# Two decoder layers on one core: one stationary tile for the new tokens' high and low rows, and an opening of layer 0 in a fixed order

## The chip, the core and the metric

The kernel runs on one core of one Trainium2 chip. The metric is device time in microseconds (us) of one launch. Five engines work beside each other, each with its own queue of instructions in a fixed order: TensorE (PE) does the matrix products, ScalarE (ACT), VectorE (DVE) and GpSimd (POOL) do element-wise work, SyncE (SP) issues most of the DMA transfers; ACT issues some too. An instruction that waits holds up everything behind it in its queue.

## The reference

Two layers of a hybrid decoder, for 1024 prompt rows and 8 new tokens, 1024 channels. Each layer, cut to what matters here:

```python
h = rms_norm(x, norm_g)          # x / sqrt(mean(x^2) + eps) * g
(a_b, a_c, a_h, a_gate, s_q, s_k, s_v, s_gate, c_u, c_v, c_gate,
 d_q, d_k, d_v, d_gate) = split(h @ w_in)
# A: short gated convolution      B: sliding-window attention (s_q, s_k rotated; s_v)
# C: u * (tril(W_s) LN(v) + b)    D: dilated attention in three groups (d_q, d_k rotated; d_v)
branches = stack([y_a*silu(a_gate), y_b*silu(s_gate), y_c*silu(c_gate), y_d*silu(d_gate)])
x = x + sum(sigmoid(h @ w_merge) * (branches @ w_branch)) @ w_out
```

Everything is float32. The outputs are the last rms_norm of x for both request groups and the updated caches; the layer-normed rows of `c_v` of the new tokens are an output too.

## The kernel before

A product of full precision is made of three: each operand is split into a high part, rounded to the fast format of PE, and a low part, the rest; high x high, low x high and high x low are added in PSUM (`mm_cols`, and L372, L375, L376 in `tm_group`). A weight tile is split by `split_w`: two buffers for the raw load (`wr`), ACT takes the high part (`wh`, L154), POOL subtracts for the low part (`wl`, L156).

The activations stand channel-major: for each of 8 k tiles of 128 channels a tile of 1032 columns, first the 8 new tokens, then 1024 prompt rows. For layer 0 the scaled input is `h0h_k` (high) and `h0l_k` (low); 1/rms is not in them, since it is a factor per row that can be applied behind the products.

The opening of layer 0 makes these tiles (L250 to L265). The input comes in row tiles (`xin0` to `xin7`, `xs` for the new tokens). For three groups of row tiles (`GROUPS`: 0 to 2 with the new tokens, 392 columns; 3 to 5, 384; 6 and 7, 256) and each k, PE transposes the blocks into a PSUM tile (L259, L262), DVE copies them to `xT0_k` (L264), and `split_x` makes the high part on ACT (L207) and the low part on DVE (L209) or, for k = 1 and 5, by ACT and POOL (L213, L214). ACT then issues the store of `xT0` to `xres` (L267) and squares the input rows with a sum (L272) for the root mean squares. The first two channel-major products, `kB` and `qB0` (`rope_products`, L277 to L281), follow. The square root and the reciprocal give `rtok` (L325, L326); for the rotation tables 1/rms is spread over the partitions by products of a matrix of ones with diagonal tiles `dg` (L327 to L338).

Token-major products (`tm_group`) have the activations as the stationary operand: for 8 blocks of 128 rows and a ninth of the 8 new tokens, 24 products each. There are three such groups in a layer: the first v group (256 columns), `c_v` (384) and the second v group (256). ACT evicts each tile with the factor `rtok` (L391, L419).

PSUM tiles: `acc` has three buffers, `ms` three, `sc` one of two banks. A scheduler orders the instructions by their operands and places, so that the order of the program is not that of the queues; where the code says so, an instruction is kept in program order. Loads issued by `load` are held back to a few marked products ahead (`mark`).

## Time and profile before

| | us |
|---|---|
| median of three runs | 2382.03 |
| the three runs | 2382.03, 2385.53, 2381.37 |
| the profiled execution | 2387.34 |
| its span in the trace | 2385.6 |
| PE busy in the span | 2365.5 |
| DVE, POOL, ACT busy | 895.2, 843.5, 687.4 |

The rows come from one profiled execution, whose own time is 5.3 us over the median of the others. Its span is 1.7 us shorter than its time. A busy PE is not one at full rate: the granted clock is told beside the stretches where it counts. Starts of PE's instructions that follow each other are a better measure of a product's price than its duration, since products overlap.

### The profile page before, as it was taken

The page shows a single profiled execution, that of the slowest core. Times are in us where ns is not written, and L with a number is a line of the kernel's source. Part 1 is how long each engine was busy: PE and PEld are TensorE (multiplying, and loading weights), DVE is VectorE, ACT ScalarE, POOL GpSimd, SP SyncE. Part 2 cuts the span into 40 slices and gives each one's busy share as a digit, 9 for nine tenths or more (in the row PEclk, how much of TensorE's full clock was granted, in tenths as well). Part 3 has the DMA queues.
Part 4 walks back from the last instruction along what each step waited for, and adds up shares of the span by engine and source line. Part 5 has one row for each costly group of instructions (what it writes and reads, how often), then busy time and mean ns, then how long its engine had stood idle before and what let it go on. Part 6 is the DMA issues. An engine that isn't in the chain of part 4 may idle for free.

```text
span 2385.6 us, 38754 instructions
## 1 busy us (share of the span) xinstructions
PE 2365.5 (99%) x15896; PEld 2305.1 (97%) x15896; DVE 895.2 (38%) x1938; ACT 687.4 (29%) x1522; POOL 843.5 (35%) x556
## 2 busy tenths in 40 slices
PE   7999999999999999999999999999999999999999
PEld 6999999999999999999999999999999999999999
DVE  4345466335312222324333455554452221213143
ACT  5133432223212222223322244323231221212243
POOL 3333234432223444434442322353322233444330
PEclk9999999999899999999999999999989999999999
DMA  7342423433322212224542423244442122222232
GB/s 237 98 123 79 119 69 109 132 102 106 100 71 88 77 55 97 64 70 123 150 146 72 145 72 98 69 151 113 111 126 67 58 91 66 98 67 62 75 99 101
DMA packets 295962, 235.82 MB, mean 99 GB/s; under 512 B 52756, under 2 KB 279696, under 8 KB 293416
## 3 DMA queue, kind: packets, MB, share of 16 engines
q1 hardware_dynamic: 267952, 206.25, 28.8%
q10 hardware_dynamic: 27832, 27.10, 4.1%
q8 instruction: 124, 2.03, 0.4%
q14 instruction: 54, 0.44, 0.1%
HBM read 192.35 MB, written 76.47 MB: 113 GB/s over the span
## 4 chain that ended last, share of the span: by engine, by line
PE 98%; DVE 1%; DMA 0%; ACT 0%; SPq 0%; issue 0%; ACTq 0%; DVEq 0%
PE acc L181 27%; PE acc L182 27%; PE acc L178 27%; PE acc L372 2%; PE acc L375 2%; PE acc L376 2%; PE sc L540 2%; PE ms L569 2%; PE ms L558 1%; PE ms L733 1%; PE ms L479 0%; PE ms L1042 0%; DMA wr<-in_w_in_dram 0%; DVE xT L264 0%; DVE h0l L209 0%; PE ms L333 0%
## 5 line engine op out<-in xcount | busy, mean ns | idle before, releaser
L156 POOL TENSOR_TENSOR wl<-wr,wh 128x384 fp32r<-128x384 f32 (+2 forms) x228 | 476.9, 2093 | 827.3 <-ACT wh L154 698.7
L181 PE MATMUL acc<-h1l,wh 128*128 128x344 f32 x1584 | 511.5, 323 | 0.0
L182 PE MATMUL acc<-h0h,wl 128*128 128x344 f32 x1584 | 510.4, 323 | 0.0
L178 PE MATMUL acc<-h0h,wh 128*128 128x344 f32 x1584 | 509.3, 322 | 0.9 <-DVE xT L264 0.9
L178 PE MATMUL acc<-h1h,wh 128*128 128x344 f32 x1584 | 510.2, 322 | 0.0
L182 PE MATMUL acc<-h1h,wl 128*128 128x344 f32 x1584 | 509.5, 322 | 0.0
L181 PE MATMUL acc<-h0l,wh 128*128 128x344 f32 x1584 | 508.9, 321 | 0.0
L154 ACT ACTIVATE wh<-wr 128x384 fp32r<-128x384 f32 (+2 forms) x228 | 205.2, 901 | 421.4 <-PE acc L181 393.6
L1005 DVE TENSOR_TENSOR th<-acc,rr 128x344 f32<-128x344 f32 x192 | 99.1, 516 | 553.5 <-PE acc L182 553.5
L181 PEld LDWEIGHTS acc<-h1l,wh 128*128 128x128 f32 x1584 | 299.9, 189 | 4.2 <-issue 3.6
L181 PEld LDWEIGHTS acc<-h0l,wh 128*128 128x128 f32 x1584 | 299.2, 189 | 3.9 <-issue 3.5
L182 PEld LDWEIGHTS acc<-h1h,wl 128*128 128x128 f32 x1584 | 299.7, 189 | 2.8 <-issue 2.3
L178 PEld LDWEIGHTS acc<-h0h,wh 128*128 128x128 f32 x1584 | 299.1, 189 | 2.8 <-issue 1.2
L182 PEld LDWEIGHTS acc<-h0h,wl 128*128 128x128 f32 x1584 | 298.6, 189 | 2.9 <-issue 2.3
L178 PEld LDWEIGHTS acc<-h1h,wh 128*128 128x128 f32 x1584 | 299.6, 189 | 1.4 <-issue 1.0
L1011 POOL TENSOR_TENSOR mg<-mg,th 128x344 f32<-128x344 f32 x144 | 134.0, 931 | 303.3 <-DVE th L1010 303.3
L1006 ACT ACTIVATE th<-th 128x344 f32<-128x344 f32 x192 | 94.3, 491 | 496.9 <-DVE th L1005 496.4
L178 PE MATMUL acc<-yh,wh 128*128 128x344 f32 x576 | 184.4, 321 | 0.0
L182 PE MATMUL acc<-yh,wl 128*128 128x344 f32 x576 | 184.3, 320 | 0.0
L181 PE MATMUL acc<-yl,wh 128*128 128x344 f32 x576 | 184.1, 320 | 0.0
L181 PE MATMUL acc<-ml,wh 128*128 128x344 f32 (+3 forms) x384 | 123.2, 321 | 0.0
L182 PE MATMUL acc<-mh,wl 128*128 128x344 f32 (+3 forms) x384 | 123.0, 321 | 0.0
(278 smaller groups left out, 3256.6 us busy)
## 6 DMA issues: line engine op xcount, KB each, us to landing
wr<-in_w_merge_dram SPq DMA_DIRECT2D x64, 512.0 KB
out_dram<-in_cache_dil_kv_dram SPq DMA_DIRECT2D x128, 255.9 KB
wr<-in_w_in_dram SPq DMA_DIRECT2D x60, 512.0 KB
y<-yscr SPq DMA_DIRECT2D x18, 516.0 KB
wr<-in_w_branch_dram SPq DMA_DIRECT2D x48, 192.0 KB
wr<-in_w_in_dram SPq DMA_DIRECT2D x32, 256.0 KB
wr<-in_w_out_dram SPq DMA_DIRECT2D x16, 512.0 KB
out_dram<-in_cache_dil_kv_dram SPq DMA_DIRECT2D x16, 511.0 KB
```

The costliest lines, as they stand in the source:

```text
L154: act.activation(hi, raw, AF.Copy)
L156: pool.tensor_tensor(lo, raw, hi.bitcast(F32), op=ALU.subtract)
L178: mm = pe.matmul(ps[:, :n], hi[:, k], xh[k][:, cs], start=(k == 0), stop=False)
L181: pe.matmul(ps[:, :n], hi[:, k], xl[k][:, cs], start=False, stop=False)
L182: pe.matmul(ps[:, :n], lo[:, k], xh[k][:, cs], start=False, stop=(k == kt - 1))
L372: mm = pe.matmul(ps[:M, :N], lh, hi[:, k % kk], start=(k == 0), stop=False)
L375: pe.matmul(ps[:M, :N], ll, hi[:, k % kk], start=False, stop=False)
L376: pe.matmul(ps[:M, :N], lh, lo[:, k % kk], start=False, stop=(k == KT - 1))
L540: pin(pe.matmul(ps[:, h, a * 256:a * 256 + u.nk], u.qs[h], u.ks[h], start=True, stop=True))
L1005: dve.tensor_tensor(t, pg[:, :CH], rr[:, cs], op=ALU.mult)
L1006: act.activation(t, t, AF.Tanh, scale=0.5)
L1011: pool.tensor_tensor(mg[m][:, cs], mg[m][:, cs], t, op=ALU.add)
```

## The change

Four things change.

The first is in `tm_group`. The ninth tile of a group, for the 8 new tokens, uses a stationary tile `hd` of 40 rows for each k: rows 0 to 7 the high parts, rows 32 to 39 the low parts, zeros between. Two products per k (weight high, weight low) give both. ACT copies the lower rows (32 to 39) out of PSUM into `sd`, DVE adds the upper ones, and the consumer reads the sum.

The second is the order of the opening, written as turns (one k of one group) and steps, all of it kept in program order. The products of the first weight tile follow the turns two behind; those of the second come four k tiles later. The high part is scaled out of PSUM directly; for even k ACT copies the tile to `xT0` afterwards, for odd k DVE copies first; all low parts are DVE's. `busy` issues products of ones, whose result nobody reads, ahead of the first turns. Six of the squares and the first splits of v weights lie between the turns.

The third is the place of the `dg` products: behind the first v group. The fourth are small moves: the load of `wsp`, transposes pinned in program order, `attention()` ahead of the scores of the D decode, three first loads on ACT's queue.

```diff
+    def tm_weights(l, srcs, kk, k0):
...
-        act.activation(hi, raw, AF.Copy)
+        in_order(act.activation(hi, raw, AF.Copy))
...
+    idle = pacc()
+    def busy(n):
+        for _ in range(n):
+            in_order(pe.matmul(idle[:, :P], onesm, onesm, start=True, stop=True))
...
-    for n0, n1 in GROUPS:
+    def turn(n0, n1, k):
...
-        for k in range(KT):
-            ps = pmisc() if k % 2 else pacc()
...
-            dve.tensor_copy(xt, ps[:, :w])
-            split_x(0, k, cs, xt, (hh, hl), k % 4 != 1)
+        ps = pmisc()
...
+        if k % 2:
+            in_order(dve.tensor_copy(xt, ps[:, :w]))
+        split_x(0, k, cs, ps[:, :w], (hh, hl))
+        if k % 2 == 0:
+            in_order(act.activation(xt, ps[:, :w], AF.Copy))
...
+    def first_products(a, s):
+        c, k = s // KT, s % KT
+        if k == 0 and a == 0:
+            if c == 1:
+                accs.append([pacc(), pacc()])
+            else:
+                two = pscore()
+                accs.append([two[:, 0], two[:, 1]])
...
+        if k == KT - 1:
+            done.append(lambda: in_order(act.activation(kq0[a][:, cs], ps, AF.Copy)))
+
+    LAG = 4
+    squares = (7, 9, 12, 14, 17, 19)
+    for s in range(3 * KT + LAG):
+        if s == 0:
+            for t in turns[:2]:
+                turn(*t[0], t[1])
+                busy(4)
+            split_first(0, 0)
+        if s in (2, 3, 6):
+            split_first(*{2: (0, 1), 3: (1, 0), 6: (1, 1)}[s])
+        if s + 2 < len(turns):
+            turn(*turns[s + 2][0], turns[s + 2][1])
+        while done:
+            done.pop(0)()
+        if s in (18, 22):
+            w_v.append(tm_weights(0, V_FIRST, 4, 4 * len(w_v)))
+        if s in squares:
+            square(squares.index(s))
+        if s < 3 * KT:
+            first_products(0, s)
+        if s >= LAG:
+            first_products(1, s - LAG)
+    for n in range(6, 9):
+        square(n)
+    while done:
+        last = done.pop(0)()
+    opening[0] = False
+    behind_opening = ExitStack()
+    behind_opening.enter_context(tc.issue_after(last.ins))
     for k in range(KT):
         act.dma_start(xres[0][k], xT0[k])
...
+                if n == 8:
+                    for k in range(KT):
+                        for a, w in enumerate(ws[k // kk]):
+                            pe.matmul(ps[:40, :N], hd[:, k], w[:, k % kk], start=(k + a == 0), stop=(k + a == KT))
+                    s = tp.tile([NS, MIX], F32, tag="ct", name="sd", bufs=4)[:, :N]
+                    act.activation(s, ps[32:32 + NS, :N], AF.Copy)
+                    dve.tensor_tensor(s, s, ps[:NS, :N], op=ALU.add)
+                    consumer(n, M, s)
+                    break
...
+        hd = sm.tile([P, KT, 40], F32R, tag="hd", name="hd")
+        pool.memset(hd.bitcast(F32), 0.0)
+        for k in range(KT):
+            for a, h in enumerate((hh, hl)):
+                pool.tensor_copy(hd[:, k, 32 * a:32 * a + NS], h[k][:, 0:NS])
...
+        tm_v(V_FIRST, 0, w_v if l == 0 else None)
+        behind_opening.close()
...
         kB, qB = rope(kq[0]), [rope(kq[1])]
-        tm_v([(S_V, P), (D_V, P)], 0)
```

How the order of the queues changes at three places:

PE, end of the first v group of layer 0; before, the first of the 24 products with 8 rows behind the last block of 128 (`acc_826` is the tile of the new tokens):

```order
L372 MATMUL acc_799<-wh_606,h0h_7_135 128x256
L375 MATMUL acc_799<-wh_606,h0l_7_143 128x256
L376 MATMUL acc_799<-wl_608,h0h_7_135 128x256
L372 MATMUL acc_826<-wh_599,h0h_0_128 8x256
L375 MATMUL acc_826<-wh_599,h0l_0_136 8x256
L376 MATMUL acc_826<-wl_601,h0h_0_128 8x256
L372 MATMUL acc_826<-wh_599,h0h_1_129 8x256
```
After, the last of 16 products with 40 rows, then the first `dg` products and the next channel-major tile:

```order
L464 MATMUL acc_809<-wh_509,hd_571 40x256
L464 MATMUL acc_809<-wl_511,hd_571 40x256
L464 MATMUL acc_809<-wh_509,hd_571 40x256
L464 MATMUL acc_809<-wl_511,hd_571 40x256
L523 MATMUL ms_834<-dg_835,onesm_85 128x8
L523 MATMUL ms_841<-dg_842,onesm_85 128x128
L198 MATMUL acc_897<-h0h_0_131,wh_892 128x344
L201 MATMUL acc_897<-h0l_0_139,wh_892 128x344
L202 MATMUL acc_897<-h0h_0_131,wl_894 128x344
```
The 8-row products give way to 40-row ones, and the `dg` products, which before stand inside the first v group's first tile, come behind the group.

ACT, end of the opening; before, from the squares to the first `rr` (`rtok` needs all squares):

```order
L272 ACTIVATE junk_341,sq0_340<-xin6_120 128x1024
L272 ACTIVATE junk_341,sq0_340<-xin7_122 128x1024
L272 ACTIVATE junk_341,sq0_340<-xs_96 8x1024
L325 ACT_TABLE_LOAD
L325 ACTIVATE rtok_521<-sq0_340,epst_91 128x8
L154 ACTIVATE wh_859<-wr_856 128x1024
L281 ACTIVATE kB_358<-acc_464 128x344
L325 ACTIVATE rtok_521<-sq0_340,epst_91 8x1
L154 ACTIVATE wh_959<-wr_957 128x768
L281 ACTIVATE qB0_359<-acc_490 128x344
L336 ACTIVATE rr_520<-ms_526 128x8
```
After, from the last scaling (`h0h_138`) to the first evictions of v tiles (`vn`):

```order
L227 ACTIVATE h0h_138<-ms,gcol 128x256
L162 ACTIVATE wh<-wr 128x1024 x2
L351 ACTIVATE kB<-sc 128x344
...
L315 ACTIVATE junk,sq_155<-xs 8x1024
L162 ACTIVATE wh<-wr 128x768
L351 ACTIVATE qB_176<-sc 128x344
L383 DMA xres_94<-xT_0_147 128x1032
...
L383 DMA xres_94<-xT_7_154 128x1032
L437 ACT_TABLE_LOAD
L437 ACTIVATE rtok<-sq_155,epst 128x8
L437 ACTIVATE rtok<-sq_155,epst 8x1
L498 ACTIVATE vn_591<-acc,rtok 128x256 x3
```
The stores of `xres`, which before stand between the scalings, now stand ahead of the table load, `rtok` and the evictions of the v group.

DVE, in the opening, first group of row tiles; before, the first copies and low parts:

```order
L264 COPY xT0_0_144<-acc_152 128x392
L209 SCALAR_TENSOR_TENSOR h0l_0_136<-xT0_0_144,gcol_93,h0h_0_128 128x392
L264 COPY xT0_1_145<-ms_160 128x392
L264 COPY xT0_2_146<-acc_170 128x392
L209 SCALAR_TENSOR_TENSOR h0l_2_138<-xT0_2_146,gcol_93,h0h_2_130 128x392
L264 COPY xT0_3_147<-ms_178 128x392
L209 SCALAR_TENSOR_TENSOR h0l_3_139<-xT0_3_147,gcol_93,h0h_3_131 128x392
```
After, from k = 5 to the start of the second group:

```order
L305 COPY xT0_5_152<-ms_245 128x392
L229 SCALAR_TENSOR_TENSOR h0l_5_144<-ms_245,gcol_93,h0h_5_136 128x392
L229 SCALAR_TENSOR_TENSOR h0l_6_145<-ms_256,gcol_93,h0h_6_137 128x392
L445 TENSOR_SCALAR nsink_564<-sink6_565 128x6
L305 COPY xT0_7_154<-ms_270 128x392
L229 SCALAR_TENSOR_TENSOR h0l_7_146<-ms_270,gcol_93,h0h_7_138 128x392
L229 SCALAR_TENSOR_TENSOR h0l_0_139<-ms_286,gcol_93,h0h_0_131 128x384
```
Low parts now read the PSUM tile, every second turn has no copy on DVE, and `nsink`, which needs the load of the sinks, stands between the low part of k = 6 and the copy of k = 7 (before: behind all the copies, the 43rd instruction).

## Rows read from the trace of the kernel before

**Rows 1.** The page, busy time by engine (us, share, instructions) and chain by engine.

```profile
PE 2365.5 (99%) x15896; PEld 2305.1 (97%) x15896; DVE 895.2 (38%) x1938; ACT 687.4 (29%) x1522; POOL 843.5 (35%) x556
...
PE 98%; DVE 1%; DMA 0%; ACT 0%; SPq 0%; issue 0%; ACTq 0%; DVEq 0%
```

**Rows 2.** Waits of PE over the span: us in total, times, longest us.

```profile
PE ms L333 <- DVE dg L332: 3.8, 3, 1.5
```

**Rows 3.** Waits of PE, 1190 to 1262 us, start of layer 1.

```profile
PE ms L333 <- DVE dg L332: 0.9, 1, 0.9
```

**Rows 4.** Timeline of PE, two token-major groups of layer 0: start us, us, engine, line, operation.

```profile
127.55 0.34 PE L372 MATMUL acc<-wh,h0h 128*8 128x384 f32 x1
...
131.53 0.34 PE L376 MATMUL acc<-wl,h0h 128*8 128x384 f32 x1
...
166.47 0.28 PE L376 MATMUL acc<-wl,h0h 128*128 128x256 f32 x1
166.59 0.28 PE L372 MATMUL acc<-wh,h0h 128*8 128x256 f32 x1
...
169.34 0.49 PE L465 MATMUL ms<-ident,wsp 128*128 128x128 f32 x3
```

**Rows 5.** Groups of ACT, 0 to 70 us: form, count | busy us, mean ns | idle before.

```profile
L154 ACT ACTIVATE wh<-wr 128x1024 fp32r<-128x1024 f32 x5 | 5.2, 1047 | 0.2 <-DMA wr<-in_w_in_dram 0.2
L207 ACT ACTIVATE h0h<-xT,gcol 128x392 fp32r<-128x392 f32 x8 | 4.9, 618 | 7.4 <-DVE xT L264 7.4
...
L207 ACT ACTIVATE h0h<-xT,gcol 128x256 fp32r<-128x256 f32 x8 | 3.8, 498 | 3.0 <-DVE xT L264 3.0
...
L281 ACT ACTIVATE kB<-acc 128x344 f32<-128x344 f32 x3 | 1.3, 440 | 0.0
```

**Rows 6.** Groups of DVE: 0 to 70 us; the last row is the page's, whole span.

```profile
L264 DVE COPY xT<-acc 128x392 f32<-128x392 f32 x4 | 2.2, 558 | 7.9 <-PE acc L262 7.9
...
L1005 DVE TENSOR_TENSOR th<-acc,rr 128x344 f32<-128x344 f32 x192 | 99.1, 516 | 553.5 <-PE acc L182 553.5
```

**Rows 7.** Timeline of PE in the opening of layer 0.

```profile
17.56 0.42 PE L262 MATMUL acc<-ident,xin 128*128 128x128 f32 x1
17.77 0.42 PE L262 MATMUL ms<-ident,xin 128*128 128x128 f32 x1
...
27.23 0.40 PE L178 MATMUL acc<-h0h,wh 128*128 128x344 f32 x1 [0.94 <-DVE xT L264]
...
50.42 0.28 PE L372 MATMUL acc<-wh,h0h 128*128 128x256 f32 x1
...
65.02 0.61 PE L333 MATMUL ms<-dg,onesm 128*128 128x128 f32 x4
```

**Rows 8.** Timeline of ACT (ACTq: its DMA issues) in the opening of layer 0.

```profile
9.48 0.62 ACT L207 ACTIVATE h0h<-xT,gcol 128x392 fp32r<-128x392 f32 x1 [1.87 <-DVE xT L264]
...
24.45 0.35 ACTq L267 DMA_DIRECT2D xres<-xT  x1
...
47.24 1.06 ACT L272 ACTIVATE junk<-xs 8x1024 f32<-8x1024 f32 x1
...
48.41 1.28 ACT L325 ACT_TABLE_LOAD   x1
49.71 0.30 ACT L325 ACTIVATE rtok<-sq,epst 128x8 f32<-128x8 f32 x1
```

**Rows 9.** Timeline of SP's DMA issues (SPq).

```profile
27.18 0.34 SPq L93 DMA_DIRECT2D sink<-in_attn_sinks_dram  x1
```

**Rows 10.** Stretches: us, busy us of PE, PEld, DVE, ACT, POOL, granted clock, DMA share, GB/s.

```profile
52.20:56.80 4.60, 1.76 (x15) 1.69 (x15) 3.67 (x5) 0.53 (x3) 3.24 (x3) 1.00 0.46 130
56.80:60.20 3.40, 3.40 (x19) 3.40 (x18) 0.29 (x1) 0.00 (x0) 0.00 (x0) 0.50 0.97 241
...
15.90:22.70 6.80, 4.95 (x21) 3.94 (x21) 6.11 (x13) 4.17 (x8) 0.92 (x2) 0.50 1.12 274
```

**Rows 11.** Timeline of DVE, the layer norm of the C branch, layer 0.

```profile
167.83 0.54 DVE L458 TENSOR_TENSOR vcs<-vcs,lngb 8x384 f32<-8x384 f32 x1
```

More of the change, by code (lines that the diff above doesn't have):

```diff
@@ L146, in copy_piece, with in_order @@
             load(*pieces.pop(), 2)
+    opening = [True]
+    def in_order(ins):
+        if opening[0]:
+            tc.keep_in_program_order(ins)
+        return ins
     def split_w(shape, dmas):
@@ L231, in load_x, with load_first @@
             xin.append(xb)
+    idle = pacc()
+    def busy(n):
+        for _ in range(n):
+            in_order(pe.matmul(idle[:, :P], onesm, onesm, start=True, stop=True))
     xs = slot("xs")[:NS, :DM]
+    w_first = [wp.tile([P, KT, P], F32, tag="wr", name="wr", bufs=2) for _ in range(2)]
+    def load_first(t, q):
+        ks_ = slice(4 * q, 4 * q + 4)
+        if t == 0:
+            sp.dma_start(w_first[0][:, ks_], win_cols(0, S_K, P)[:, ks_])
+            return
+        for h in range(2):
+            sp.dma_start(w_first[1][:, ks_, h * 64:(h + 1) * 64], win_cols(0, S_Q + 192 * h, 64)[:, ks_])
     for q in range(2):
@@ L240 @@
             if q == 0 and n == 0:
-                sp.dma_start(xs, i["x_sample"].rearrange("b s d -> (b s) d"))
-                sp.dma_start(gcol, i["norm_g"].rearrange("l (k p) -> p l k", p=P))
-    w_first = [w_std(win_cols(0, S_K, P), KT)]
+                act.dma_start(xs, i["x_sample"].rearrange("b s d -> (b s) d"))
+                act.dma_start(gcol, i["norm_g"].rearrange("l (k p) -> p l k", p=P))
+        load_first(0, q)
+    for q in range(2):
+        load_first(1, q)
     load_x(3, 8)
@@ L254 @@
         w = cs.stop - cs.start
[L255 to L265 removed]
+        ks_ = slice(k * P, (k + 1) * P)
@@ new lines, in turn @@
+        ps = pmisc()
+        if off:
+            in_order(pe.transpose(ps[:, 0:NS], xs[:, ks_], ident[:NS, :NS]))
+        for n in range(n0, n1):
+            c0 = off + (n - n0) * P
+            in_order(pe.transpose(ps[:, c0:c0 + P], xin[n][:, ks_], ident))
+        xt = xT0[k][:, cs]
+        if k % 2:
[3 more added lines that the diff above has]
+            in_order(act.activation(xt, ps[:, :w], AF.Copy))
+    sq0 = sm.tile([P, 9], F32, tag="sq0", name="sq0")
@@ new lines, with square, split_first @@
+    junk = slot("junk")
+    def square(n):
+        src, M = (xin[n], P) if n < 8 else (xs, NS)
+        return in_order(act.activation(junk[:M, :DM], src[:M, :DM], AF.Square, accum_out=sq0[:M, n:n + 1]))
+    busy(18)
+    kq0 = [slot("kB"), slot("qB0")]
+    turns = [(g, k) for g in GROUPS for k in range(KT)]
+    wf = [[wp.tile([P, KT, P], F32R, tag=t, name=t, bufs=4) for t in ("wh", "wl")] for _ in range(2)]
+    w_v = []
+    done = []
+    def split_first(a, q):
+        ks_ = slice(4 * q, 4 * q + 4)
+        raw = w_first[a][:, ks_]
+        hi, lo = [t[:, ks_] for t in wf[a]]
+        in_order(act.activation(hi, raw, AF.Copy))
+        pool.tensor_tensor(lo, raw, hi.bitcast(F32), op=ALU.subtract)
@@ L266 @@
+    for n in range(6, 9):
[5 more added lines that the diff above has]
+    behind_opening.enter_context(tc.issue_after(last.ins))
     for k in range(KT):
         act.dma_start(xres[0][k], xT0[k])
-    sq0 = sm.tile([P, 9], F32, tag="sq0", name="sq0")
-    junk = slot("junk")
-    for n in range(9):
-        src, M = (xin[n], P) if n < 8 else (xs, NS)
-        act.activation(junk[:M, :DM], src[:M, :DM], AF.Square, accum_out=sq0[:M, n:n + 1])
@@ L405, in tm_v @@
                 act.dma_start(dst, vsam[:, c0:c0 + P])
+        tm_v(V_FIRST, 0, w_v if l == 0 else None)
+        behind_opening.close()
+        for n0, n1 in ((8, 9), (0, 4), (4, 8)):
+            ps = pmisc()
+            M = NS if n0 == 8 else P
+            for n in range(n0, n1):
+                dg = sm.tile([P, P], F32, tag="dg", name="dg", bufs=2)
+                dve.tensor_scalar(dg[:M, :M], ident[:M, :M], rtok[:M, n:n + 1], None, op0=ALU.mult)
+                tc.keep_in_program_order(pe.matmul(ps[:, (n - n0) * P:(n - n0) * P + M], onesm[:M], dg[:M, :M],
+                                                   start=True, stop=True))
+            cs = slice(0, NS) if n0 == 8 else slice(NS + n0 * P, NS + n1 * P)
+            w = cs.stop - cs.start
+            act.activation(rr[:, cs], ps[:, :w], AF.Copy)
+            dve.tensor_tensor(cosT[:, cs], cosT[:, cs], rr[:, cs], op=ALU.mult)
+            pool.tensor_tensor(sinT[:, cs], sinT[:, cs], rr[:, cs], op=ALU.mult)
         kB, qB = rope(kq[0]), [rope(kq[1])]
-        tm_v([(S_V, P), (D_V, P)], 0)
         qB.append(rope_tile(w_pair(l, S_Q, 1), "qB1"))
@@ L443 @@
         bsps = [lngb[:, 6 * P:7 * P], lngb[:, 7 * P:8 * P], wsps[:, 6 * P:7 * P]]
+        load(wsp, i["w_spatial"][l].rearrange("g t s -> t g s"), 2)
         for h in range(2):
@@ L459 @@
         store_later(2, o["chunk_v_s"][l].rearrange("b s c -> (b s) c"), cvs)
-        load(wsp, i["w_spatial"][l].rearrange("g t s -> t g s"), 2)
         wsT = dec([P, 6, P], "wsT")
```

77 lines of the change are left out of this document (34 added, 43 removed).

## The prediction

> **What bounds the kernel now.** I read the busy shares and the chain of waits first, then who TensorE (PE) waits for, then the opening row by row. PE is busy 2365.5 of 2385.6 us and 98% of the chain that ended last is PE's own work [rows 1]. So the time is PE's list of products, plus about 20 us in which PE has nothing to do, plus what the lower clock costs. Behind the inputs that the opening of layer 0 waits for, the largest wait of PE is for `dg` at L333, the diagonal tiles that spread 1/rms over the partitions: 3.8 us in three waits [rows 2]. One of these, 0.9 us, is in layer 1 and the only one at that layer's start [rows 3]; the other two stand in the opening. Three things can therefore move the time: fewer products, the opening, and the one wait in layer 1. The rest that the diff moves lies under a PE that never stops.
>
> **Part 1, the joint stationary tile.** A token-major group ends with 24 products for the 8 new tokens: rows high, rows low, rows high again, by 8 k tiles. The last such group of layer 0 runs from 166.59 to 169.34, 2.75 us or 0.1146 each; the group of 384 columns starts its 24 at 127.55 and the last one at 131.53, 0.173 each [rows 4]. The price goes by the columns that pass, not by the rows that stand: the product of 128 rows just ahead, at 166.47, takes 0.12. With rows high and rows low side by side in a tile of 40 rows, 16 products do what 24 did. Per layer that saves 8 x 0.1146 twice and 8 x 0.173 once, 3.22 us; for two layers **6.4 us**. Added are, for each of the six groups, one ScalarE (ACT) copy out of PSUM (0.44 us at 344 columns [rows 5]) and one VectorE (DVE) addition (0.52 [rows 6]), and per layer a memset and 16 small copies on GpSimd (POOL). PE goes on into another accumulator meanwhile and waits for none of it, so I cost them at nothing. Without that cover they would cost 1 us a group, 6 us in all. A tile of 40 rows could cost more than one of 8 only if the rows mattered, which 8 against 128 excludes.
>
> **Part 2, the `dg` products behind the first group.** In layer 1 about 25 us of products now lie between the first use of `rtok` and `dg`. The 0.9 us go: **0.9 us.** What is late next would be `rtok` itself, for the eviction of the first v tile, but PE has three accumulators, 8 us of products, before it needs that eviction. In layer 0 the two waits are part of the opening's sum.
>
> **Part 3, the opening.** I compare one mark: the fourth tile of the first v group can begin, 72 of its products done and no `dg` counted. Before, it comes when a pair of `dg` products starts at 65.02 (four records, two passes each, in 0.61 us with their tail [rows 7]); six `dg` products of about 0.2 us had run by then, so the mark is 65.0 - 1.2 = **63.8**, idle time and half clock included.
>
> After, ACT sets the pace. In a turn of even k, ACT scales the transposed tile out of PSUM into `h0h`, DVE takes the low part, and only then ACT copies the same tile to `xT0` (DVE and ACT read the tile in turn). In a turn of odd k DVE copies first and ACT waits for that. So a pair of turns is a chain: scale 0.62, low part 0.52 (the DVE row with one operand in PSUM), copy 0.44 to 0.5, scale 0.62, less the overlap of a start with the end before it: 2.2 us at 392 and 384 columns, 1.75 at 256 [rows 5, 6]. Twelve pairs: 8 x 2.2 + 4 x 1.75 = 24.6. Between the turns ACT also has four half splits (0.55 each, half of the 1024-column row), two 1024-column splits of the v weights (1.0), four evictions of `kB` and `qB0` (0.42), and six squares at a pitch of 1.17 (47.24 to 48.41 [rows 8]): 2.2 + 2.0 + 1.7 + 7.0 = 12.9. From the first scaling to the last that is 37.5 us if nothing else is waited for.
>
> It starts at about 8.6: before, the first scaling began at 9.48 behind a 0.56 us copy [rows 8, 6], and after it needs no copy. The 18 `busy` products ahead of it take two passes of 0.21 each at the lower level (17.56 to 17.77 [rows 7]), 7.6 us from about the first microsecond, so they end about when the inputs are there; the eight later ones lie in gaps. Three waits can be added. `nsink` now stands in DVE's queue between two turns of the first group and needs the load of the sinks, which SP issues behind the inputs (before: at 27.18 [rows 9]); the changed SP order brings it earlier, to some time behind the seventh input tile, and I put 0 to 4 us. The fifth step's product for the second weight tile waits until ACT has evicted the other half of the same two-bank tile: 0 to 1.5. The first low weights come from POOL: 0 to 2. I take 2.4 of these 7.5, since part of ACT's other work fills them. So the last scaling ends at 8.6 + 37.5 + 2.4 = 48.5.
>
> Behind it ACT still does, in this order, since nothing overtakes in its queue: second v split 0.95; split of the next q weights, whose buffer POOL frees late, 2.8 with its wait; eviction 0.43; three squares 3.5; a split of 768 columns 0.83; eviction 0.43; eight issues of `xres` at 0.35 [rows 8], 2.8; the table load 1.30; `rtok` 0.30 and the reciprocal with its way back 0.35; and the first eviction of a v tile, 0.47. Sum 14.2, so that the fourth v tile has its accumulator at 62.7. PE waits for that: after the last scaling it has some 15 products of 0.155 and 72 of 0.117 to do, 10.7 us, and arrives at 59.2. The wait of 3.5 us stands in the place of the two `dg` waits of before. What follows a wait of this size is in the rows: after 52.2 to 56.8, where PE was busy 1.76 of 4.6 us, the granted clock was 0.50, the 1.2 GHz level, from 56.8 to 60.2 [rows 10]. 3.4 us at half the rate cost 1.7. The mark after is 62.7 + 1.7 = 64.4, the opening **0.6 us worse**.
>
> On the table load the trace and a page differ. The load begins at 48.41, directly behind the last square, and `rtok` at 49.71: 1.30 us in all [rows 8]. The Trainium skill (ScalarE: Activation LUTs, What ACT_TABLE_LOAD costs) adds a drain of 1380 ns to each switch. No row here shows it; with it the mark would be 65.8 and the forecast 2376.7.
>
> The smaller moves cost nothing by the trace. `ident` goes from SP's queue to ACT's with `xs` and `gcol`, ahead of everything. The load of `wsp` and the transposes pinned in order have no wait of PE in the rows of before. If the transposes of `cvs` came up too early they would wait for the layer norm of the new rows, which ended at 168.37 [rows 11], 1.0 us ahead of the `wsp` transposes that they now follow directly [rows 4]; its loads no longer stand behind `qB2`, so it should be earlier by more than PE is. Without that, PE would wait for that row, at most the 2 or 3 us that DVE is late.
>
> **Sum.** 6.4 + 0.9 - 0.6 = 6.7 us less. Against the profiled execution, 2387.3, that is 2380.6; this execution stood 5.3 over the median of the three runs, 2382.0, so the forecast is **2375.3**.
>
> **Rivals.**
> *The waits are absorbed.* ACT's own work in the opening, without the low part in each chain (12 x 0.52) and without the three waits, is 31 us, and PE's is 64 transposes of about 0.11 (0.21 at half clock) and 144 products of 0.16 (23.2 us from 27.23 to 50.42) [rows 7], 30. Then the last scaling ends at 40 and the mark comes 8 or 9 us earlier: net 15, 2367, with 2362 to 2371 around it. For it: squares and splits lie between the chained steps and DVE has room. Against it: the order of ACT's queue is fixed, and the chains are data, not chance.
>
> *The clock alternates in the opening.* Between 15.9 and 22.7 PE was busy 4.95 of 6.8 us at a granted clock of 0.50 [rows 10], in a stretch where it ran in short bursts and waited between them. The changed opening has 30 us of full-rate work in 37 to 40, in bursts with a gap at each step. At the lower level a step takes 60 / 24 = 2.5 us against ACT's 1.56, so PE becomes the pace and loses 0.38 us for each us at that level. Three stretches of 3.4 us cost 3.9: 2379, with 2377 to 2386 for a total of 5 to 28 us at that level. The Trainium skill (TensorE: Matmul & The Clock Gate, A second HAM failure mode: psum-queue depth-cycling) tells of just such switching where PE pauses briefly between groups; by that rule the time would be 2379.
>
> *Slower: the lower clock holds through the opening.* Then PE's 60 us set the pace, the last scaling comes at about 67 instead of 48.5, and the mark some 18.5 us later, 19 with the 0.6: 6.4 + 0.9 - 19 is a loss of 11.8, 2394. It decides against the change from 30 us at the lower level on (30 x 0.38 = 11.5 eats the 6.7 and 4.8 more). For it: no stretch of the opening is without gaps. Against it: at that level PE has no gaps left, and from 56.8 to 60.2 it was busy without a gap, 3.40 of 3.40 us at 0.50 [rows 10], ahead of the full-rate products around 65.
>
> **How the numbers follow.** The forecast case (2372 to 2378) has a chance of 0.42, absorbed waits 0.22, the alternating clock or longer waits 0.24, slower 0.12. 0.2% of 2382 is 4.8 us, about what a measurement can tell from no change: faster is under 2377.3, slower over 2386.8. Faster: 0.22 and 0.37 of the first case, 0.59. Same: 0.29. Slower: 0.12. The range from 2363 to 2386 leaves out the slower case and a part of the best one.
>
> **What would show it.** In the profile after: 40-row products, 16 to a group, at 0.115 and 0.173 us apart; no wait for `dg` in either layer; a wait of 2 to 6 us at the fourth v tile, ended by an ACT eviction; ACT nearly full from 9 to 49 us; the last scaling at 46 to 51; the mark at 62 to 67. I am wrong if the last scaling ends by 43 or after 53, if PE never waits at the fourth v tile, or if a wait over 2 us appears behind 75 us.

## The result, and the profile after

| | before | after |
|---|---|---|
| median of six runs, us | 2385.66 | 2402.26 |
| lowest and highest, us | 2381.37 to 2395.06 | 2400.56 to 2406.30 |
| span of the profiled execution, us | 2385.6 | 2401.6 |

The ratio of the times is 1.0072, with a 95% interval of 1.0058 to 1.0086. The change makes the kernel 17 us (0.7%) slower, outside the range of the prediction and on the other side.

The page of the changed kernel, busy time by engine and the chain by engine, answers to [rows 1]:

```profile
PE 2370.8 (99%) x15900; PEld 2312.9 (96%) x15900; DVE 897.9 (37%) x1938; ACT 697.3 (29%) x1540; POOL 846.7 (35%) x586
...
PE 90%; DMA 3%; issue 2%; DVE 2%; ACT 1%; POOL 1%; ACTq 1%; POOLq 0%; DVEq 0%; SPq 0%
```

PE is busy 5.3 us longer although it has less useful work; some of the new products are those of ones, some run at the lower clock. The chain is PE's own for 90% of the span, where it was 98%. What PE waits for (us in total, times, longest) answers to [rows 2]:

```profile
PE acc L473 <- ACT vn L498: 13.2, 3, 9.7
PE sc L345 <- ACT wh L329: 3.4, 1, 3.4
PE sc L345 <- ACT kB L351: 2.7, 1, 2.7
PE ms L802 <- DVE sd L785: 2.3, 2, 1.4
```

No wait for `dg` is left in either layer. In its place stand 13.2 us for the evictions of v tiles, `vn`, and 2.3 for `sd`. This `sd` is a tile of the D decode, its scores, reduced by DVE at L785; the sum of the joint tile's halves has the same name but is made at L467, and PE waits for it nowhere. The two waits at L345 stand in the opening, among the first products.

The timeline of ACT in the opening shows how the largest wait comes about. It answers to [rows 8].

```profile
10.77 1.28 ACT L227 ACT_TABLE_LOAD   x1 [10.77 <-DMA gcol<-in_norm_g_dram]
12.07 0.59 ACT L227 ACTIVATE h0h<-ms,gcol 128x392 fp32r<-128x392 f32 x1
...
52.98 0.48 ACT L227 ACTIVATE h0h<-ms,gcol 128x256 fp32r<-128x256 f32 x1
...
62.71 0.86 ACTq L383 DMA_DIRECT2D xres<-xT  x2
63.35 0.44 ACT L351 ACTIVATE qB<-sc 128x344 f32<-128x344 f32 x1
63.61 7.95 ACTq L383 DMA_DIRECT2D xres<-xT  x6
71.59 1.28 ACT L437 ACT_TABLE_LOAD   x1 [7.80 <-DMA xres<-xT]
72.88 0.48 ACT L437 ACTIVATE rtok<-sq,epst 128x8 f32<-128x8 f32 x2
73.45 0.84 ACT L498 ACTIVATE vn<-acc,rtok 128x256 f32<-128x256 f32 x2
```

The first scaling waits for `gcol`, whose load is now on ACT's queue: 12.07 where it was 9.48. The last scaling ends at 53.46. Of the eight issues of `xres` the last six take 7.95 us, and the table load, `rtok` and every eviction stand behind them. PE has meanwhile filled its three accumulators; its timeline at the fourth v tile, and at the same kind of wait in the second v group:

```profile
73.98 0.58 PE L473 MATMUL acc<-wh,h0h 128*128 128x256 f32 x1 [9.66 <-ACT vn L498]
...
176.09 0.58 PE L473 MATMUL acc<-wh,h0h 128*128 128x256 f32 x1 [2.60 <-ACT vn L498]
```

The stretches around both waits (us, busy us of PE, PEld, DVE, ACT, POOL, granted clock, DMA share, GB/s) answer to [rows 10]:

```profile
64.00:68.00 4.00, 0.32 (x3) 0.12 (x1) 0.00 (x0) 0.00 (x0) 1.33 (x1) 1.00 1.00 348
68.00:72.00 4.00, 0.00 (x0) 0.00 (x0) 0.00 (x0) 0.41 (x1) 0.00 (x0) 0.70 1.02 386
72.00:76.00 4.00, 2.02 (x9) 2.02 (x10) 0.74 (x4) 2.56 (x6) 0.00 (x0) 0.50 1.02 402
76.00:80.00 4.00, 4.00 (x21) 4.00 (x20) 0.00 (x0) 0.48 (x1) 0.00 (x0) 0.52 0.21 73
80.00:84.00 4.00, 4.00 (x36) 4.00 (x35) 0.00 (x0) 0.47 (x1) 0.00 (x0) 1.00 0.11 38
...
175.00:180.00 5.00, 3.91 (x18) 3.91 (x19) 3.36 (x4) 0.95 (x2) 1.16 (x1) 0.54 0.66 207
180.00:185.00 5.00, 5.00 (x36) 4.99 (x36) 0.00 (x0) 0.76 (x2) 0.00 (x0) 0.78 0.59 174
```

While ACT issues, the 16 DMA engines are full (share 1.00 to 1.02), and from 64.3 on PE does nothing. It comes back at 73.98 at 0.50, the 1.2 GHz level: 21 products from 76 to 80, 36 from 80 to 84. About 5.7 us behind the wait run at half the rate, which costs 2.8. The second wait is followed by 6.8 us at 0.50 (found in narrower windows), at most 3.4 us more.

**The ledger.** The mark of the prediction, 63.8 before, is after 73.98 + 2.8 = 76.8: 13.0 us later. The second v group of layer 0 adds 2.6 and up to 3.4, that of layer 1 a third wait for `vn`, 0.9; the waits for `sd` in the D decode 2.3, those for `pn` there 0.8. Saved are 6.4 by the joint tile and 0.9 for `dg` in layer 1. Together 15.7 of the 16.0 us by which the spans differ. The other stretches at the lower clock behind the opening, 30.8 us long in all before and 27.3 after, are not in this sum.

### The profile page after: what moved, and what is told of

It is laid out like the page before. It is cut to its first block, busy times and chain, and to the rows that moved or that the text cites. A ratio compares the mean times of both kernels' runs of the same rounds, so it can differ in the third digit from the quotient of the medians.

```text
span 2401.6 us, 38812 instructions
## 1 busy us (share of the span) xinstructions
PE 2370.8 (99%) x15900; PEld 2312.9 (96%) x15900; DVE 897.9 (37%) x1938; ACT 697.3 (29%) x1540; POOL 846.7 (35%) x586
## 4 chain that ended last, share of the span: by engine, by line
PE 90%; DMA 3%; issue 2%; DVE 2%; ACT 1%; POOL 1%; ACTq 1%; POOLq 0%; DVEq 0%; SPq 0%
PE acc L201 26%; PE acc L198 26%; PE acc L202 26%; PE sc L662 2%; PE ms L691 2%; PE ms L680 1%; PE acc L473 1%; PE acc L476 1%; PE acc L477 1%; DMA wr<-in_w_in_dram 1%; PE ms L855 1%; DMA vscr<-vn 1%; DMA qb<-qscrB 1%; POOL wl L164 0%; PE ms L601 0%
## 5 line engine op out<-in xcount | busy, mean ns | idle before, releaser
L164 POOL TENSOR_TENSOR wl<-wr,wh 128x384 fp32r<-128x384 f32 (+2 forms) x226 | 469.2, 2078 | 827.2 <-ACT wh L162 754.3
L198 PE MATMUL acc<-h0h,wh 128*128 128x344 f32 x1536 | 494.9, 322 | 0.0
L201 PE MATMUL acc<-h0l,wh 128*128 128x344 f32 x1536 | 493.7, 321 | 0.0
L202 PE MATMUL acc<-h0h,wl 128*128 128x344 f32 x1536 | 493.6, 322 | 0.0
L201 PEld LDWEIGHTS acc<-h0l,wh 128*128 128x128 f32 x1536 | 290.0, 189 | 3.7 <-issue 3.3
L198 PEld LDWEIGHTS acc<-h0h,wh 128*128 128x128 f32 x1536 | 289.6, 189 | 2.6 <-issue 2.2
L202 PEld LDWEIGHTS acc<-h0h,wl 128*128 128x128 f32 x1536 | 289.8, 189 | 1.7 <-issue 1.3
```

Source lines behind the costliest of these rows:

```text
L164: pool.tensor_tensor(lo, raw, hi.bitcast(F32), op=ALU.subtract)
L198: mm = pe.matmul(ps[:, :n], hi[:, k], xh[k][:, cs], start=(k == 0), stop=False)
L201: pe.matmul(ps[:, :n], hi[:, k], xl[k][:, cs], start=False, stop=False)
L202: pe.matmul(ps[:, :n], lo[:, k], xh[k][:, cs], start=False, stop=(k == kt - 1))
```

## The experiments

**Theories.** The first, Q in the expectations, is that the row of `xres` issues behind the opening holds ACT's queue and by that PE. Rivals: the opening's chain itself is longer than costed (start, chain, squares); the small moves (M), or the joint tile's eviction and addition, cost what was put at nothing; the copies of the caches (D), which take part of the DMA engines' time near 160 to 175, hold up ACT's stores of the second v group. Each time here is a median; each ratio is against the kernel before, run beside it.

### The opening as a whole: old_open, old_open_no_hd, no_hd

`old_open` is the changed kernel with the opening of before (turns, steps and `busy` out, loads back on SP); joint tile, `dg` and small moves stay.

> The changed kernel with the opening of before (its order, its loads, its place of the squares and of the stores of xres); joint tile, dg behind the first v group and small moves stay. Theory O (the loss is the fixed opening's; the rest of the change is worth the 7.3 us of the sum): 2376 to 2380, ratio 0.996 to 0.998, no wait over 1.5 us behind 75 us. Rival T (as the joint tile alone, 5 us slower than before, shows, PE's saved time turns into waits in the second v group and the decode whatever the opening): 2384 to 2392, with 2 to 5 us of waits at the second v group.

`old_open_no_hd` also takes the joint tile out, `no_hd` takes only the joint tile out of the changed kernel:

```diff
-                if n == 8:
-                    for k in range(KT):
-                        for a, w in enumerate(ws[k // kk]):
-                            pe.matmul(ps[:40, :N], hd[:, k], w[:, k % kk], ...
...
-        hd = sm.tile([P, KT, 40], F32R, tag="hd", name="hd")
```

> As old_open, and with the 24 products of 8 rows instead of the joint tile: only dg behind the first v group and the small moves. Theory O: 6.4 us over old_open, within 2 of before less the 0.9 to 3 us of dg. Rival T: within 2 us of old_open, since the joint tile brings nothing that reaches the end.

> The changed kernel with 24 products of 8 rows instead of the joint tile, all else as changed. If the joint tile is worth its 6.4 us in the changed kernel: 2408 to 2409. If its gain is given back in the waits behind 95 us (2.6 us at 176 with the lower clock, 1.4 at 420): those waits shrink and the time is 2400 to 2404.

Measured: `old_open` 2380.36, ratio 0.9983 [0.9973, 0.9992], faster than both kernels, with no wait for `vn` over 0.3 us and none behind 75 us over 1.7 (for the decode's `sd`); `old_open_no_hd` 2389.92, 1.0017 [1.0008, 1.0026]; `no_hd` 2417.50, 1.0127 [1.0112, 1.0142]. So the fixed opening costs 21.9 us (2402.26 - 2380.36), and without it the rest of the change gains 4.8. The joint tile is worth 9.6 us with the old opening and 15.2 with the new one, more than the 6.4 that its products save and more than either expectation for `no_hd`. In `no_hd` the rest is waits that the changed kernel doesn't have: all idle time of PE together is 37.0 us, against 26.7. Its largest, in total:

```profile
PE acc L464 <- ACT vn L483: 9.7, 1, 9.7
PE sc L647 <- DVE dqp L413: 5.9, 2, 5.0
```

### The row of issues: xres_turns

```diff
             in_order(act.activation(xt, ps[:, :w], AF.Copy))
+        if n1 == 8:
+            in_order(act.dma_start(xres[0][k], xT0[k]))
...
-    for k in range(KT):
-        act.dma_start(xres[0][k], xT0[k])
```

> The changed kernel with each store of xres issued in the last turn of its k, as its tile gets complete, and none ahead of the table load. Theory Q (the eight issues in a row took 8.8 us there, not 2.8, because the DMA was full): the table load begins by 67 instead of 71.6, PE's wait of 9.7 us for the first v eviction falls under 4, the lower clock from 69 to 80 goes or shrinks to 3.4 us, and the time falls from 2402 by 8 to 13. Rival C (the chain of turns, squares and splits is late by itself): the wait stays over 6 us, since the issues only move to another place of the same queue, and the time falls by less than 4.

Measured: 2395.11, 1.0038 [1.0025, 1.0052], 7.2 us less than the changed kernel. The same eight stores, now spread over the last group of turns, take 0.33 to 0.38 us each; the last of them, and then the table load and the fourth v tile:

```profile
55.83 0.38 ACTq L310 DMA_DIRECT2D xres<-xT  x1
...
66.78 1.28 ACT L437 ACT_TABLE_LOAD   x1
```
```profile
69.17 0.39 PE L473 MATMUL acc<-wh,h0h 128*128 128x256 f32 x1 [2.23 <-ACT vn L498]
```

The table load comes directly behind the last eviction, the wait falls from 9.66 to 2.23, and no stretch from 66 to 80 is at the lower clock. Theory Q holds: it is the row of issues that keeps ACT, and by it PE. The gain is a little short of the 8 to 13 us expected: the eight issues now stand among the turns, so that the last scaling comes 3.2 us later (56.13), and the wait of the second v group grows from 2.60 to 3.70.

An issue took 0.33 to 0.38 us in these turns and 1.3 us (7.95 / 6) in the row, about the time in which its 516 KB pass. Full DMA engines alone don't explain that. In the changed kernel a store of a v tile (128 KB) was issued in 0.33 us while they were as full as in the row; in the kernel before, one such store took 4.70 us while they were nearly idle, with a cache copy under way that SP had issued at 62.96. First the one in the changed kernel, then the one in the kernel before, each with its stretch (columns as above):

```profile
73.96 0.33 ACTq L500 DMA_DIRECT2D vscr<-vn  x1
73.96:74.29 0.33, 0.31 (x1) 0.31 (x2) 0.04 (x1) 0.33 (x2) 0.00 (x0) 0.50 1.02 400
```
```profile
65.73 4.70 ACTq L393 DMA_DIRECT2D vscr<-vn  x1
65.73:70.43 4.70, 4.70 (x42) 4.70 (x41) 0.00 (x1) 0.00 (x0) 0.00 (x0) 1.00 0.16 64
```

What stretches an issue is therefore open. The 4.70 us cost nothing, since PE was busy throughout.

### The start: gcol_sp

```diff
-    act.dma_start(ident, c["ident"])
+    sp.dma_start(ident, c["ident"])
...
-                act.dma_start(xs, i["x_sample"].rearrange("b s d -> (b s) d"))
-                act.dma_start(gcol, i["norm_g"].rearrange("l (k p) -> p l k", p=P))
+                sp.dma_start(xs, i["x_sample"].rearrange("b s d -> (b s) d"))
+                sp.dma_start(gcol, i["norm_g"].rearrange("l (k p) -> p l k", p=P))
```

> The changed kernel with ident, xs and gcol loaded on SP's queue as before. First scaling now at 12.07 because ACT waits for gcol until 10.77. Theory S (the late start moves the whole opening): first scaling at 9 to 9.5, last one 2.5 to 3 us earlier than 53.5, the time 2 to 5 us less than 2402. Rival (absorbed): the chain waits elsewhere in the first group (nsink, inputs, the two-bank tile), the last scaling moves by under 1 us and the time by under 1.5.

Measured: 2403.14, 1.0067 [1.0049, 1.0086]: no gain, though the start is what it was made to be. ACT at the start, PE at the fourth v tile:

```profile
5.50 1.28 ACT L227 ACT_TABLE_LOAD   x1 [5.50 <-DMA gcol<-in_norm_g_dram]
...
8.47 0.59 ACT L227 ACTIVATE h0h<-ms,gcol 128x392 fp32r<-128x392 f32 x1 [1.68 <-PE ms L302]
```
```profile
72.11 0.58 PE L473 MATMUL acc<-wh,h0h 128*128 128x256 f32 x1 [10.01 <-ACT vn L498]
```

The first scaling moves from 12.07 to 8.47, so the loads on ACT's queue were the late start. The last scaling (50.78) is only 2.2 us earlier, since the earlier chain now runs into the load of the sinks, one of the three waits that the prediction listed. DVE stands at `nsink`, where it didn't in the changed kernel:

```profile
25.18 0.16 DVE L445 TENSOR_SCALAR nsink<-sink 128x6 f32<-128x6 f32 x1 [4.01 <-DMA sink<-in_attn_sinks_dram]
```

Of the 2.2 us, 1.9 reach the fourth v tile, where the row of issues again ends the wait; that is about what the intervals of the two kernels leave open. The start mended alone can't be seen in the time.

### Three holdups of the opening: xres_gcol_acc, and the squares: squares_end

`xres_gcol_acc` joins the last two edits and gives each pair of first products two accumulators instead of two halves of one tile:

```diff
-            if c == 1:
-                accs.append([pacc(), pacc()])
-            else:
-                two = pscore()
-                accs.append([two[:, 0], two[:, 1]])
+            accs.append([pacc(), pacc()])
```

> The changed kernel with three mends of its opening: xres stored in the last turns, ident, xs and gcol on SP's queue, and every pair of first products in two accumulators of their own instead of the two banks of one tile (in the changed kernel PE waits 2.7 us at 31.8 for the eviction of the other bank, and the lower clock follows). Theory (these three waits are serial, each moves the rest): the last scaling 5 to 7 us earlier than in xres_turns (56.5), the fourth v tile begins at 61 to 65 instead of 69.2, the time 4 to 7 us under the 2395 of xres_turns. Rival (one chain of ACT and DVE paces the opening, waits are made up within it): the fourth v tile begins by 67 at the earliest, the time within 2.5 of 2395.

`squares_end` is that kernel with the six squares between the turns moved behind them:

```diff
-    squares = (7, 9, 12, 14, 17, 19)
+    squares = ()
...
-    for n in range(6, 9):
+    for n in range(9):
```

> xres_gcol_acc with all nine squares behind the chain of turns. Theory A (ACT's list paces the opening, as the prediction has it): the last scaling 5 to 7 us earlier than 51.4, the table load no earlier than 58 to 61 (59.3 there), so that the fourth v tile now waits for its accumulator for 3 to 6 us where it did not wait before, with time 2390 to 2395. Rival P (PE paces it): the last scaling less than 3 us earlier and PE waits over 5 us for the first eviction.

Measured: `xres_gcol_acc` 2389.96, 1.0011 [0.9999, 1.0023]; `squares_end` 2397.84, 1.0057 [1.0039, 1.0076]. In the first, no wait is left at the fourth v tile, and the first score product of B starts at 129.1, where it stood at 131.8 before and 143.1 after. That is no lead over the opening of before: up to that product the joint tile and `dg` save time too, and `old_open`, which has both with the old opening, reaches it at 127.1. So the fixed opening with three holdups out is still 2.0 us behind; a fourth is left, 3.5 us of DVE at `nsink`. And the second v group has its wait:

```profile
161.97 0.39 PE L469 MATMUL acc<-wh,h0h 128*128 128x256 f32 x1 [2.93 <-ACT vn L494]
```

In `squares_end` the last scaling starts at 48.25 instead of 50.98. Six squares of 1.17 us out of the chain make it 2.7 earlier, not 7.0. By its figures rival P came true, but PE, busy 33.4 of the 39.4 us from the first scaling to the last, doesn't set the pace. DVE waits longer for the sinks, whose load comes later in this run:

```profile
26.61 0.16 DVE L441 TENSOR_SCALAR nsink<-sink 128x6 f32<-128x6 f32 x1 [5.04 <-DMA sink<-in_attn_sinks_dram]
```

From `nsink` to the last scaling it is 21.6 us where it was 25.8 (25.18 to 50.98): 4.2 of the 7.0; where the rest went is not followed here. Behind the turns all squares count: the table load comes at 63.37 instead of 59.27, and PE waits ahead of a v tile for the eviction of `qB0`, which stands behind squares:

```profile
63.41 0.58 PE L469 MATMUL acc<-wh,h0h 128*128 128x256 f32 x1 [6.13 <-ACT qB L349]
```

### The wait of the second v group: late_copies, after_late, before_late, old_open_late

In the changed kernel ACT stands still there between two evictions. Its timeline:

```profile
167.89 0.48 ACT L498 ACTIVATE vn<-acc,rtok 128x256 f32<-128x256 f32 x1 [2.89 <-PE acc L477]
172.27 0.33 ACTq L500 DMA_DIRECT2D vscr<-vn  x1
...
175.56 0.47 ACT L498 ACTIVATE vn<-acc,rtok 128x256 f32<-128x256 f32 x1 [7.20 <-DMA vscr<-vn]
```

The eviction ends at 168.37, its store is issued at 172.27. In the trace the store waits for a completion counter that it shares with an earlier transfer, a cache copy of 508 KB which SP issued at 162.44 and which has nothing to do with v. The copy's last landing on that counter is at 172.19:

```profile
162.44 0.69 SPq L93 DMA_DIRECT2D out_dram<-in_cache_dil_kv_dram  x1
```

The cache copies are issued one for each load behind the eighth. All four kernels start them later, and differ in what they stand on: `xres_gcol_acc`, the changed kernel, the kernel before, `old_open`.

```diff
-        if pieces and nload[0] > 8:
+        if pieces and nload[0] > 20:
```

> xres_gcol_acc with the cache copies held back by twelve more weight loads, so that none stands among the loads and stores of layer 0's second v group. Theory D (ACT's store of a v tile and its copy to the output wait, issue by issue, for an unrelated earlier DMA, a cache copy of 508 KB or a weight load, and hold up the next eviction): the wait of 2.9 us at 162 goes or falls under 1 and the time falls by 2 to 5 from 2390. Rival (the burst of loads for the layer norm and the weights alone fills the DMA): the wait stays over 2 us, time within 1.5 of 2390.

> The changed kernel with the cache copies held back by twelve more weight loads. Theory D (the changed kernel's wait of 2.6 us at 176 and the lower clock behind it come from evictions that stand behind stores which wait for a cache copy): that wait goes, 5 to 9 us under 2402, and the 9.7 us at the first v group stay. Rival (the late opening alone makes the second group's loads late): the wait stays, time within 2 of 2402.

> The kernel before with the cache copies held back by twelve more weight loads. If the collision is one that the change brought (before has no wait there): within 1.5 us of before. If the copies cost the kernel before as well, by the lower clock or by waits: 2 to 6 us less than before, and then held-back copies are a gain of their own that says nothing about the change.

> old_open with the cache copies held back by twelve more weight loads. If what both bring adds up: 2373 to 2378, ratio 0.9955 to 0.997. If old_open has nothing left at the second v group (it has no wait there): within 1.5 us of 2380.4.

| kernel | median, us | ratio | against its own base, us |
|---|---|---|---|
| `late_copies` | 2381.55 | 0.9984 [0.9975, 0.9993] | -8.4 |
| `after_late` | 2397.88 | 1.0041 [1.0023, 1.0059] | -4.4 |
| `before_late` | 2388.92 | 1.0009 [0.9997, 1.0022] | +3.8 |
| `old_open_late` | 2388.43 | 1.0009 [0.9998, 1.0020] | +8.1 |

Where the second v group of layer 0 waited, the wait goes: in `after_late` it is gone while the 9.8 at the fourth v tile stays (first row), in `late_copies` all 2.9 go. What is left there stands in layer 1 (second row), as the second wait of the first row does (1.90 at 1334.3).

```profile
PE acc L473 <- ACT vn L498: 11.7, 2, 9.8
```
```profile
1316.69 0.39 PE L469 MATMUL acc<-wh,h1h 128*128 128x256 f32 x1 [1.44 <-ACT vn L494]
```

So the copies hold up ACT in the changed kernel. The 4.4 us fall just short of the 5 to 9 expected; the 8.4 us of `late_copies` are more than its wait of 2.9, and where the rest lies isn't shown. Where that wait did not exist, the same edit makes a new one: in `before_late` for the eviction of `kB`, in `old_open_late` at the same place.

```profile
PE acc L178 <- ACT kB L281: 4.3, 1, 4.3
```
```profile
PE acc L198 <- ACT kB L302: 3.2, 1, 3.2
```

The two gains don't add: `old_open` and `late_copies` reach 2380.4 and 2381.6, their sum is worse than either. `before_late` can't be told from the kernel before (its interval holds 1); the 8.1 us of `old_open_late` are clear. They are more than the 3.2 for `kB`: in the two profiled executions PE's idle time is 5.3 us longer in all (23.6 against 18.3), and the mean granted clock of the runs is 0.9925 against 0.9941, worth some 4 us (an estimate from these two). Why later copies do this is open.

### The joint tile alone: hd_only

The kernel before with the new branch for the ninth tile, the tile `hd` and a wider buffer for the sum:

```diff
+                if n == 8:
+                    for k in range(KT):
+                        for a, w in enumerate(ws[k // kk]):
+                            pe.matmul(ps[:40, :N], hd[:, k], w[:, k % kk], ...
```

> The kernel before with the joint stationary tile alone (40 rows, 16 products for a group's last tile). Sum theory: 6.4 us less than before, ratio 0.9973, six groups of 16 products at the same distance of 0.115 and 0.173 us. Rival, that the saved PE time turns into waits elsewhere (the added eviction and addition, or evictions and loads that PE now meets earlier): less than half of it, ratio over 0.9987, and a new or longer wait of PE behind 75 us in the rows.

Measured: 2392.04, 1.0022 [1.0011, 1.0033]: 6.6 us slower, with 48 products fewer. Two waits of PE are new:

```profile
PE ms L480 <- DMA wsp<-in_w_spatial_dram: 5.2, 2, 3.2
...
PE ms L671 <- DVE dqs L836: 3.3, 1, 3.3
```

The `wsp` transposes stood at 169.34 [rows 4]. With the short ninth tile the scheduler puts them where their load has not landed yet:

```profile
153.97 0.77 PE L480 MATMUL ms<-ident,wsp 128*128 128x128 f32 x5 [1.96 <-DMA wsp<-in_w_spatial_dram]
```

So the edit that saves 6.4 us of products loses 6.6; the two new waits are 8.5 of these 13.0 us. The first comes from the order that the scheduler then chooses: the changed kernel pins the transposes; `small_back`, below, unpins them and has the same wait. That the second, for `dqs`, is of the same kind is not shown.

### The small moves: small_back, old_open_sc

`small_back` is the changed kernel with the load of `wsp`, the unpinned transposes and `attention()` where they were. `old_open_sc` is `old_open` with the scores of the D decode ahead of `attention()` again:

```diff
-        attention()
         decD.scores(0, dqs[0], dks[0])
+        attention()
```

> The changed kernel with the small moves taken back: the load of wsp behind the layer norm, the spatial and decode transposes not pinned, the scores of the D decode ahead of attention(). Theory M (these moves make the waits behind 95 us: 2.6 us at 176 with 6.8 us of lower clock, 1.4 at 420, 0.9 and 0.8 in others): these waits go, 5 to 9 us less than 2402. Rival (they follow from the later opening and the shifted turns of the DMA queues): the wait of 2.6 us stays or reappears within 10 us of its place, time within 3 of 2402.

> old_open with the scores of the D decode again ahead of attention(), everything else as there. In old_open PE waits 3.0 us in two places for sd of the decode and 0.8 for pn. Theory (this move makes those waits): they go, 2 to 4 us less than 2380.4, ratio to before 0.9965 to 0.9975. Rival (the decode's DVE work is late anyway, or the waits come back as one for dqs): within 1.5 us of 2380.4 or slower.

Measured: `small_back` 2404.10, 1.0073 [1.0054, 1.0093], which can't be told from the changed kernel; `old_open_sc` 2384.65, 0.9992 [0.9982, 1.0001], 4.3 above `old_open` by the medians but not clearly apart from it by the ratios. Theory M falls as an account of the time. The move of `attention()` does make the decode's waits for `sd` and `pn`: with it taken back they are gone, but others come. First `small_back`, then `old_open_sc`:

```profile
PE ms L587 <- DMA wsp<-in_w_spatial_dram: 5.9, 2, 3.2
```
```profile
PE ms L686 <- DVE dqs L851: 4.5, 2, 3.8
```

## Why the prediction was wrong, step by step

**The price of the joint tile was right at its place.** The first and the last of the 16 products with 40 rows, and the `dg` products that follow directly, answer to [rows 4]:

```profile
90.92 0.28 PE L464 MATMUL acc<-wh,hd 128*40 128x256 f32 x1
...
92.65 0.28 PE L464 MATMUL acc<-wl,hd 128*40 128x256 f32 x1
92.86 0.38 PE L523 MATMUL ms<-dg,onesm 8*128 8x8 f32 x2
```

They stand (92.65 - 90.92) / 15 = 0.115 us apart, and those of 384 columns 0.175 (140.21 to 142.83). What failed is taking 6.4 us as its worth in the kernel: 9.6 and 15.2 gained, and 6.6 lost, were measured, by what surrounds it.

**The `dg` step was right.** Neither layer waits for `dg`. (In the trace of before its products are spread from the first tile of the v group to the start of the fourth, 53.62 to 65.02, not in the first alone.) From the first product of layer 1 (1197.8 before, 1216.1 after) to the end the change gains 2.3 us, against 4.1 costed for that layer's joint tile and `dg`; the difference is that layer's waits for `vn` and `sd`, 0.9 each.

**The added eviction and addition cost PE nothing, as forecast; a small move did not.** No wait of PE is for the copy at L466 or the sum at L467. The decode's `sd`, which PE does wait for, is another tile, with 128 rows and not 8. Its waits, 2.3 us, and those for `pn`, 0.8, come with `attention()` ahead of the scores of the D decode, one of the moves that "cost nothing by the trace":

```profile
419.63 0.38 PE L802 MATMUL ms<-ident,sd 128*8 128x128 f32 x2 [1.39 <-DVE sd L785]
```

**The opening failed, in three of its terms.** Of the 12.4 us between the mark forecast (64.4) and the mark found (76.8):

- The start, 3.5: first scaling at 12.07, not 8.6. The loads moved to ACT's queue were among the moves put at nothing; `gcol` landed at 10.77, and at 5.50 from SP's queue in `gcol_sp`. The 8.6 itself was right for that queue (8.47).
- The chain, 1.5: 41.4 us from first to last scaling, 39.9 forecast. This is the part with the longest working. That its sum held is partly luck: the wait at `nsink`, put at up to 4, is absent only because the chain starts late (4.01 in `gcol_sp`); the wait for the two-bank tile was 2.73, with at most 1.5 allowed; PE's 3.38 us for the first weight split (to 14.97) was not on the list; and one of the two splits of the v weights stands behind the last scaling, so that the sum counts it in the chain and in the tail.
- The tail, 6.3: 20.5 us, 14.2 forecast. The eight issues of `xres` took 8.8 instead of 2.8, since 0.35 was taken from a row in which one issue stood alone [rows 8]. This is the step that decides: the path was right, PE did wait for an eviction behind ACT's queue, but this term was put at a third of its size. The Trainium skill (DMA: Bandwidth & Descriptors, Issuing engines are not separate DMA queues) calls the time that initiating a DMA takes on the sequencer "usually small relative to the DMA itself". The runs here agree for the stores spread over the turns, 0.33 to 0.38; for six in a row it was as long as the transfers.
- The clock, 1.1: 5.7 us at the lower level cost 2.8, not 1.7.

PE arrived at the fourth v tile at 73.98 - 9.66 = 64.3, which is the last scaling plus 10.9 (10.7 forecast); the wait was 9.66, not 3.5.

**Nothing behind the opening was costed.** The second v group lost 2.6 us and up to 3.4 of clock. I had followed each moved issue up to its own queue's next instruction, not to the transfers that other issues wait for. The prediction named a wait over 2 us behind 75 us as what would make it wrong, and there it is; so did a last scaling that ends after 53 (53.46).

**The rivals.** The waits were not absorbed. The alternating clock is seen, at the size it was given: 0.57 in the mean from 14 to 22 and from 32 to 36, 10.2 us at the lower level in narrower windows, and 6.8 and 3.4 us before. The two stretches of the changed kernel come with one long wait of PE each, 3.38 us (to 14.97) and 2.73 (to 31.75). So the switching that the Trainium skill tells of (TensorE: Matmul & The Clock Gate, A second HAM failure mode: psum-queue depth-cycling) is there, but not by the brief pauses between groups that it names: those from 36 to 64 left the clock full. The alternation didn't decide. The slower case came true in sign and not in mechanism: its 30 us at the lower level were never near, and from 36 to 64 PE was busy 27.45 of 28.00 us at the full clock:

```profile
14.00:22.00 8.00, 6.62 (x23) 5.07 (x24) 3.23 (x6) 4.38 (x9) 3.71 (x10) 0.57 1.02 335
...
32.00:36.00 4.00, 4.00 (x19) 3.88 (x19) 1.18 (x2) 1.91 (x4) 0.00 (x0) 0.57 0.56 211
36.00:64.00 28.00, 27.45 (x190) 25.72 (x190) 8.58 (x18) 20.38 (x41) 7.66 (x4) 1.00 0.22 55
```

**The table load** takes 1.29 us until `rtok` again (71.59 to 72.88), without the drain that the Trainium skill adds (ScalarE: Activation LUTs, What ACT_TABLE_LOAD costs).

**What stays open.** What stretches an issue; the clock outside the ledger; and why the same later copies cost `old_open` 8.1 us where nothing had waited for the early ones.

**A version that beats both** is `old_open`, 2380.36: joint tile, `dg` behind the first group and pinned small work, with the opening left as it was. It is 0.2% faster than before. `late_copies` keeps the fixed opening and is as fast, after four repairs.

## What to carry to other kernels

The time of one DMA issue that stands alone is no price for a row of them: spread stores that nobody waits for, and never put them in a row ahead of the instruction that frees the next engine's buffers. When a step is moved, follow what it displaces on its own queue and then what the other queues wait for among its transfers. And where a scheduler sets the order, removing work is only worth its price if the order around it is pinned: the same edit gave 15 us, 10 us and minus 7.

## What the runs showed of the hardware

An issue on ACT's queue took 0.33 to 0.38 us for eight stores of 516 KB spread over 12 us, and 1.3 us in the mean for six of them in a row, at 348 to 402 GB/s. ACT did nothing else meanwhile, and everything behind it waited. The engines' share alone doesn't tell the price: 0.33 us at a share of 1.02, 4.70 at 0.16, both for a store of 128 KB. A store can also wait for a transfer of another queue that has its completion counter: one stood from 168.37 to 172.27, until a cache copy had landed. A stationary tile of 40 rows costs the same as one of 8, 0.115 us at 256 columns; one of 128 rows 0.118. After a pause of 9.66 us in which PE did nothing, it ran 5.7 us at the 1.2 GHz level, although it had full work from then on. Shorter pauses went either way: behind 2.60 us in the second v group there were 6.8 us at that level, and none behind 2.23 in `xres_turns` or 2.93 in `xres_gcol_acc`.
